# Two blocks of two layers on one core: the last layer on its 256 output tokens, norm sums and the last affine on other engines, constants that wait by tile

## The chip, the core and the metric

The kernel runs on one core of a Trainium2 chip. The metric is the device time of one execution in microseconds (us), the median of several runs. Engines are named as in the profile: PE is TensorE (matmuls; PEld its weight loads), DVE is VectorE, ACT is ScalarE, POOL is GpSimd, and SP is SyncE, whose queue issues the transfers.

## What is computed

The first block is one layer of RWKV-7 and one of gated DeltaNet, each with its SwiGLU, on 256 tokens of width 1024. The second block puts 16 learnt tokens in front (272 tokens) and runs two layers; only the 256 tokens behind those 16 are the output. In short form, from the reference:

```python
x = concat([meta, x], axis=1)                        # 16 + 256 tokens
for i in range(2):
    x = layer_norm(alpha * x + 0.5 * swiglu(x, gate1, up1, down1), ln1)
    z, xbc, dt, fq, fk, fv, ff, cq, ckv, kr = split(x @ w_in)
    y = concat([ssd_mixer(z, xbc, dt), fox_mixer(fq, fk, fv, ff), mla_mixer(cq, ckv, kr)])
    x = layer_norm(alpha * x + y @ w_out, ln2)
    x = layer_norm(alpha * x + 0.5 * swiglu(x, gate2, up2, down2), ln3)
return x[:, 16:]
```

This is its meaning and not its text. The three mixers of a layer are causal: the state mixer, an attention with a forget gate ("fox") and a latent attention ("MLA"). Tokens mix nowhere else. So in the last layer the front 16 tokens are needed as keys, values and state, and not as queries, gates or rows of the later projections.

## The kernel before

Activations lie with features on the partitions, as eight tiles of 128 features by 272 tokens (256 in the first block). A float32 product is made from three: operand and weight are each split into a high and a low part, and high x high, high x low and low x high are summed in PSUM. So one block of 128 output features takes 8 x 3 = 24 matmuls (66 in a down projection of 2816 features), each as wide as the tokens.

- **Weights.** `weight` (L103) loads 128x1024 values by SP, ACT casts the high part (L108), and DVE, or POOL where `onpool` says so, subtracts to the low part (L111). Three raw buffers and four of each part go round. For the first four blocks of each SwiGLU the low parts are made on POOL (`onpool = 4`, L272).
- **SwiGLU.** `ffn` (L259): 22 pairs of gate and up blocks, two pairs at a time, by `mm3` (L149; its products are L157 to L161 for the first four blocks and L166, L167, L169 for the others), then eight blocks down, straight into a layer norm.
- **Mixer.** `mixer` (L320) projects 20 blocks of features. Four come first; the other 16 are emitted step by step by `project` (L123, matmul L137) among the steps of the gates, latents, states, attentions and the state mixer, in an order that `run_spread` (L750) makes from a list of steps and places. Each attention (`attend`, L523) goes through its units of queries: 16 queries of both heads, then 128 and 128 queries for each head. A unit passes score, turn and apply in three successive steps.
- **Output projection.** L705 to L721; four blocks first, then two and two, in two PSUM banks, with DVE reading a result for the norm at L205.
- **Layer norm.** `layer_norm` (L176). Features lie on partitions, so the mean and the mean square come from matmuls with a matrix of 1/1024 (L212, L213). Before that, POOL adds the eight chunks and their squares together (L191: `sa` the chunks, `qa` the squares, each over chunks 0 to 6), so that only the sum and the last chunk go to TensorE. Four more products that nobody reads follow (L215). Then ACT takes the square of the mean (L217), Ln and Exp (L219, L220), DVE subtracts and scales (L221, L235), and with gain and shift ACT writes the high part for the next matmuls (L242), POOL the norm's result (L249), DVE the low part (L232).
- **From the first block to the second.** The last norm of the first block also copies the 16 front tokens into its results: `front[:, k]`, on ACT (L241) and POOL (L247). `front` lies in the pool `modp`, with the modulation vectors. This pool is closed, and the pool `cst` takes its place in memory (L1730) with mask, rope tables and other constants (L297 to L312).
- **Output.** After the last norm SP stores eight tiles (L1735).

The order of work on an engine's queue is not only that of the program's text: the framework places instructions, so that a weight split or a constant can stand ahead of work that is written before it.

## Time and profile before

| | us |
|---|---|
| runs before | 2275.15, 2273.75, 2267.9 (median 2273.75) |
| span of the profiled execution | 2273.7 |
| mean granted TensorE clock, of full speed | 0.972 |
| PE busy, of the span | 2121.1 |
| DVE, ACT, POOL busy | 1415.1, 1083.4, 679.0 |

The span runs from the first to the last instruction of the profiled execution; the profile gives no time of its own outside it. A row of the timeline has the start from the beginning of the span, the duration, the engine, the line of the kernel, the operation, output and inputs; in brackets the idle time of the engine before it and what released it. Successive matmuls overlap, so what one costs is the distance between starts. In the table of stages the clock is the granted share of 2.4 GHz.

### The profile page before, as it was taken

How to read it: one execution, taken by the hardware profiler on the slowest of the kernel's cores; microseconds unless marked ns; L12 is line 12 of the kernel's file. 1: busy time of each engine (PE TensorE's matmuls, PEld its weight loads, DVE VectorE, ACT ScalarE, POOL GpSimd, SP SyncE). 2: the span in 40 equal slices, each digit the busy share in tenths (PEclk: the TensorE clock that was granted, in tenths of full speed). 3: DMA queues.
4: the chain of work that ended last, by engine and by line, in shares of the span. 5: the costliest groups of instructions: out<-in, count | busy, mean ns of one | idle time of the engine just before them, and what ended most of it. 6: DMA issues, size and time to landing. Idle time of an engine off the chain costs nothing.

```text
span 2273.7 us, 43912 instructions
## 1 busy us (share of the span) xinstructions
PE 2121.1 (93%) x17673; PEld 1954.6 (86%) x17673; DVE 1415.1 (62%) x2673; ACT 1083.4 (48%) x1955; POOL 679.0 (30%) x626
## 2 busy tenths in 40 slices
PE   5699999988978898999999999899999999998998
PEld 5488888978977787999899987699999998778998
DVE  6877675455587875654554586565455448665544
ACT  2344444334465545454444464554444536455442
POOL 1625203795464315704201310400230032022003
PEclk9799999999997999999999999999999999999999
DMA  6433222566544322765554432255446553224543
GB/s 248 141 99 115 75 75 86 204 236 214 208 152 149 127 84 88 258 201 185 159 174 165 158 117 65 93 168 176 162 146 193 172 173 115 80 84 144 177 167 112
DMA packets 102236, 337.87 MB, mean 149 GB/s; under 512 B 11472, under 2 KB 19472, under 8 KB 102032
## 3 DMA queue, kind: packets, MB, share of 16 engines
q1 hardware_dynamic: 102032, 335.07, 44.1%
q8 instruction: 138, 2.26, 0.4%
q14 instruction: 66, 0.54, 0.1%
HBM read 333.97 MB, written 1.05 MB: 147 GB/s over the span
## 4 chain that ended last, share of the span: by engine, by line
PE 59%; DVE 6%; ACT 2%; issue 2%; POOL 2%; DMA 0%; POOLq 0%; DVEq 0%; ACTq 0%
PE pj L167 14%; PE pj L166 13%; PE pj L169 13%; PE pj L137 6%; PE pj L157 1%; PE pj L158 1%; DVE wl L111 1%; PE yp L586 1%; PE pj L161 1%; PE B L1369 1%; PE sy L636 1%; PE S L547 1%; PE pt L569 0%; ACT wh L108 0%; DVE r L221 0%
## 5 line engine op out<-in xcount | busy, mean ns | idle before, releaser
L111 DVE TENSOR_TENSOR wl<-wr,wh 128x1024 fp32r<-128x1024 f32 (+2 forms) x533 | 642.7, 1215 | 399.4 <-ACT wh L108 216.7
L108 ACT CAST wh<-wr 128x1024 fp32r<-128x1024 f32 (+2 forms) x557 | 555.8, 1001 | 568.6 <-PE pj L167 206.6
L832 POOL TENSOR_TENSOR adaccp<-adaccp,adar 128x512 f32<-128x512 f32 x140 | 209.5, 1497 | 46.5 <-ACT adar L828 19.4
L202 POOL TENSOR_TENSOR x<-x,m 128x272 f32<-128x272 f32 (+1 forms) x42 | 34.5, 858 | 600.6 <-ACT m L199 600.6
L268 DVE TENSOR_TENSOR hh<-sg,pj 128x272 f32<-128x272 f32 (+1 forms) x132 | 56.6, 429 | 149.2 <-PE pj L169 126.2
L830 POOL TENSOR_SCALAR adar<-adar,cond,zcol 128x512 f32<-128x512 f32 x98 | 112.5, 1155 | 34.4 <-DMA adar<-in_ada_dram 34.4
L111 POOL TENSOR_TENSOR wl<-wr,wh 128x1024 fp32r<-128x1024 f32 x24 | 58.1, 2432 | 141.7 <-ACT wh L108 134.2
L191 POOL TENSOR_TENSOR sa<-sa,r 128x272 f32<-128x272 f32 (+1 forms) x40 | 55.6, 1390 | 126.8 <-DVE r L205 126.7
L166 PE MATMUL pj<-s0h,wh 128*128 128x272 f32 (+1 forms) x240 | 69.5, 290 | 16.4 <-ACT wh L108 16.4
L186 ACT ACTIVATE q<-r 128x272 f32<-128x272 f32 (+1 forms) x80 | 33.2, 426 | 98.9 <-DVE r L205 63.6
L167 PE MATMUL pj<-s5l,wh 128*128 128x272 f32 (+1 forms) x240 | 69.5, 290 | 0.0
L166 PE MATMUL pj<-s6h,wh 128*128 128x272 f32 (+1 forms) x240 | 69.3, 289 | 0.0
L167 PE MATMUL pj<-s2l,wh 128*128 128x272 f32 (+1 forms) x240 | 69.2, 288 | 0.0
L167 PE MATMUL pj<-s7l,wh 128*128 128x272 f32 (+1 forms) x240 | 69.2, 288 | 0.0
L167 PE MATMUL pj<-s3l,wh 128*128 128x272 f32 (+1 forms) x240 | 69.1, 288 | 0.0
L167 PE MATMUL pj<-s1l,wh 128*128 128x272 f32 (+1 forms) x240 | 69.1, 288 | 0.0
L166 PE MATMUL pj<-s3h,wh 128*128 128x272 f32 (+1 forms) x240 | 69.0, 288 | 0.0
L167 PE MATMUL pj<-s4l,wh 128*128 128x272 f32 (+1 forms) x240 | 69.0, 288 | 0.0
L169 PE MATMUL pj<-s6h,wl 128*128 128x272 f32 (+1 forms) x240 | 69.0, 288 | 0.0
L166 PE MATMUL pj<-s4h,wh 128*128 128x272 f32 (+1 forms) x240 | 69.0, 288 | 0.0
L166 PE MATMUL pj<-s5h,wh 128*128 128x272 f32 (+1 forms) x240 | 69.0, 288 | 0.0
L167 PE MATMUL pj<-s6l,wh 128*128 128x272 f32 (+1 forms) x240 | 68.9, 287 | 0.0
(1660 smaller groups left out, 7850.5 us busy)
## 6 DMA issues: line engine op xcount, KB each, us to landing
wr<-in_ffn_in_dram SPq DMA_DIRECT2D x264, 512.0 KB, 3.9
wr<-in_ffn_out_dram SPq DMA_DIRECT2D x96, 512.0 KB, 3.5
adar<-in_ada_dram SPq DMA_DIRECT2D x80, 512.0 KB, 3.7
wr<-in_w_in_dram SPq DMA_DIRECT2D x40, 512.0 KB, 3.5
wr<-in_ffn_out_dram SPq DMA_DIRECT2D x48, 384.0 KB, 3.9
wr<-in_gin_dram SPq DMA_DIRECT2D x32, 512.0 KB, 4.2
wr<-in_w_out_dram SPq DMA_DIRECT2D x16, 512.0 KB, 3.5
adaring<-in_ada_dram SPq DMA_DIRECT2D x8, 512.0 KB, 6.1
```

Source lines behind the costliest of these rows:

```text
L108: nc.scalar.copy(h, r)
L111: eng.tensor_tensor(l, r, h.bitcast(F32), op=SUB)
L137: mm(o, a, b, start=(c == 0), stop=(c == 23))
L166: mm(o, wh, xs[k][0], start=(i == 0), stop=False)
L167: mm(o, wh, xs[k][1], start=False, stop=False)
L169: mm(o, w(k)[1], xs[k][0], start=False, stop=(i == K - 1))
L186: nc.scalar.activation(q[k], d[k], AF.Square)
L191: nc.gpsimd.tensor_tensor(a, t[0] if k == 1 else a, t[k], op=ADD)
L202: nc.gpsimd.tensor_tensor(xs[i], xs[i], m0, op=SUB)
L268: nc.vector.tensor_tensor(hh, sg, up, op=MUL)
L830: nc.gpsimd.tensor_scalar(t, src, c, n.zcol, op0=MUL, op1=ADD)
L832: nc.gpsimd.tensor_tensor(acc[e], acc[e], src, op=ADD)
```

## The change

In the last layer a first token `f0 = 16` is passed to the mixer. The query blocks (MLA's latents 4 and 5, fox's 6 and 7) and the gates (16 to 19) are projected for the tokens from `f0` on, the attentions leave out the unit of 16 queries (24 steps instead of 28), the state mixer's rows, the output projection, its norm and the last SwiGLU have 256 tokens, and the output tiles are stored whole. In both layers' mixer norms the additions of `sa` are on DVE, those of `qa` stay on POOL. The affine of the last norm is on ACT. The pool of constants is opened with `reuse_waits="tile"`: its tiles wait for the tiles whose bytes they take, not for the whole pools.

```diff
-    def project(self, name, blocks, xs, T, per):
+    def project(self, name, blocks, xs, T, per, cut=lambda g: 0):
...
-            o = self.ps("pj", T)
+            t0 = cut(g)
+            o = self.ps("pj", T - t0)
...
-                    mm(o, a, b, start=(c == 0), stop=(c == 23))
+                    mm(o, a, b[:, t0:], start=(c == 0), stop=(c == 23))
...
-                    nc.gpsimd.tensor_tensor(a, t[0] if k == 1 else a, t[k], op=ADD)
+                    (sums if sums is not None and i == 0 else nc.gpsimd).tensor_tensor(a, t[0] if k == 1 else a, t[k], op=ADD)
...
-            if not split:
+            if split is None:
+                nc.scalar.activation(xn[k], d[k], AF.Identity, scale=g(k), bias=b(k))
+            elif not split:
                 nc.gpsimd.tensor_scalar(xn[k][:, f:], d[k], g(k), b(k), op0=MUL, op1=ADD)
...
-        T = T2
+        T, TQ = T2, T2 - f0
...
-                units = [(0, 0)] + [(hh, i) for i in (1, 2) for hh in range(2)]
+                units = ([] if f0 else [(0, 0)]) + [(hh, i) for i in (1, 2) for hh in range(2)]
...
-                    mm(yp[rows, s0:], xdt[:sn, i, 64 * h:64 * h + 64], m[:sn], start=(i == 0), stop=(i == 2))
+                    mm(yp[rows, e:], xdt[:sn, i, 64 * h:64 * h + 64], m[:sn], start=(i == 0), stop=(i == 2))
...
-                       (n.project(win, blocks, sp, T, 8), 384 // 8, 0, 1), 
+                       (n.project(win, blocks, sp, T, 8, lambda g: f0 if g in (4, 5, 6, 7) or g > 15 else 0), 384 // 8, 0, 1),
...
-                    outs = [n.ps(t, T) for t in ("pj", "pj", "yp", "bc")[:m]]
+                    outs = [n.ps(t, TQ) for t in ("pj", "pj", "yp", "bc")[:m]]
...
-            return n.layer_norm(out, xs, ISQ2, 0.5e-5, lambda k: P(f"ln2_g{l}", k), lambda k: P(f"ln2_b{l}", k), T,
+            return n.layer_norm(out, [x[:, f0:] for x in xs], ISQ2, 0.5e-5, lambda k: P(f"ln2_g{l}", k), lambda k: P(f"ln2_b{l}", k), TQ,
...
-                                                   bufs=2 if nm not in ("m0", "m2") else 1), (), slow=False)
+                                                   bufs=2 if nm not in ("m0", "m2") else 1), (), slow=False, sums=nc.vector)
...
-        xs, sp = self.mixer(l, xs, sp)
+        f0 = META if last else 0
+        xs, sp = self.mixer(l, xs, sp, f0)
...
-                     lambda k: P(f"ln3_g{l}", k), lambda k: P(f"ln3_b{l}", k), T, None if last else ())
+                     lambda k: P(f"ln3_g{l}", k), lambda k: P(f"ln3_b{l}", k), T - f0, None if last else ())
...
-        with tc.tile_pool(name="cst", bufs=1) as cst:
+        with tc.tile_pool(name="cst", bufs=1, reuse_waits="tile") as cst:
...
-                nc.sync.dma_start(out[k], xs[k][:, META:])
+                nc.sync.dma_start(out[k], xs[k])
```

## Rows read from the trace of the kernel before

**Rows 1.** The page: TensorE's share of the span; the chain that ended last, by engine.
```profile
PE 2121.1 (93%) x17673; PEld 1954.6 (86%) x17673; DVE 1415.1 (62%) x2673; ACT 1083.4 (48%) x1955; POOL 679.0 (30%) x626
...
PE 59%; DVE 6%; ACT 2%; issue 2%; POOL 2%; DMA 0%; POOLq 0%; DVEq 0%; ACTq 0%
```

**Rows 2.** Busy us (instructions) by stage; us, PE, PEld, DVE, ACT, POOL, clock, DMA.
```profile
1894.00:2016.00 122.00, 118.50 (x776) 92.08 (x774) 90.05 (x257) 71.45 (x176) 10.10 (x13) 1.00 0.26 85
2016.00:2070.00 54.00, 43.32 (x282) 37.59 (x281) 31.67 (x60) 27.13 (x42) 29.36 (x25) 0.94 0.31 98
2070.00:2263.00 193.00, 192.94 (x1533) 191.69 (x1531) 96.36 (x120) 87.48 (x120) 19.12 (x19) 1.00 0.49 161
2263.00:2274.00 11.00, 1.58 (x5) 0.59 (x4) 6.01 (x15) 0.63 (x2) 5.15 (x8) 0.73 0.28 96
```

**Rows 3.** Timeline, PE: start us, us, engine, line, op, operands; 272 columns, down-products' ends.
```profile
2193.55 0.29 PE L166 MATMUL pj<-h0h,wh 128*128 128x272 f32 x1
...
2259.88 0.62 PE L212 MATMUL S<-sa,ones1k 128*128 128x272 f32 x2
```

**Rows 4.** The same, PE, 256 columns, in the first block's last SwiGLU.
```profile
1019.82 0.37 PE L166 MATMUL pj<-h0h,wh 128*128 128x256 f32 x1
...
1081.95 0.60 PE L212 MATMUL S<-sa,ones1k 128*128 128x256 f32 x2
```

**Rows 5.** The same, PE, around the score of 16 queries in a fox attention.
```profile
1985.00 0.23 PE L543 MATMUL S<-cum,ident 32*32 32x16 f32 x2
...
1985.77 0.39 PE L137 MATMUL pj<-s0h,wh 128*128 128x272 f32 x1
```

**Rows 6.** Groups by line and shape, 1890 to 2030: xcount | busy us, mean ns.
```profile
L569 PE MATMUL pt<-ident,att 64*16 64x64 f32 x4 | 0.9, 219 | 0.0
```

**Rows 7.** Timeline, PE, end of the last output projection and what follows.
```profile
2045.51 0.29 PE L717 MATMUL pj<-yo3h,wl 128*128 128x272 f32 x1
2053.15 1.27 PE L212 MATMUL S<-sa,ones1k 128*128 128x272 f32 x2 [7.35 <-POOL sa L191]
```

**Rows 8.** Groups on POOL, 2030 to 2057, with idle before them.
```profile
L111 POOL TENSOR_TENSOR wl<-wr,wh 128x1024 fp32r<-128x1024 f32 x4 | 9.8, 2449 | 0.0
...
L191 POOL TENSOR_TENSOR sa<-sa,r 128x272 f32<-128x272 f32 x5 | 4.9, 977 | 0.1
...
L191 POOL TENSOR_TENSOR sa<-r,r 128x272 f32<-128x272 f32 x1 | 0.9, 908 | 11.1 <-DVE r L209 11.1
```

**Rows 9.** Groups on DVE, 2030 to 2050.
```profile
L209 DVE TENSOR_TENSOR r<-r,m 128x272 f32<-128x272 f32 x7 | 6.4, 921 | 0.1
...
L200 DVE TENSOR_TENSOR r<-r,m 128x272 f32<-128x272 f32 x1 | 0.4, 433 | 0.0
```

**Rows 10.** Timeline, ACT, the first block's last norm.
```profile
1087.78 0.30 ACT L312 CAST identR<-ident 128x128 fp32r<-128x128 f32 x1 [4.56 <-POOL x L247]
1087.99 0.38 ACT L217 ACTIVATE m<-S 128x256 f32<-128x256 f32 x1
...
1090.51 0.60 ACT L242 ACTIVATE s0h<-r,par 128x256 fp32r<-128x256 f32 x1 [0.79 <-DVE r L235]
```

**Rows 11.** The same, POOL.
```profile
1087.54 0.21 POOL L247 COPY x<-front 128x16 f32<-128x16 f32 x1
```

**Rows 12.** The same, PE.
```profile
1083.30 0.67 PE L213 MATMUL S<-q,ones1k 128*128 128x256 f32 x2
...
1091.16 0.60 PE L157 MATMUL pj<-s0h,wh 128*128 128x272 f32 x1 [4.49 <-ACT s0h L242]
...
1102.07 0.29 PE L161 MATMUL pj<-s0l,wh 128*128 128x272 f32 x1
```

**Rows 13.** Timeline, POOL, the tail.
```profile
2268.06 2.88 POOL L249 TENSOR_SCALAR x<-r,par 128x272 f32<-128x272 f32 x4 [0.39 <-DVE r L235]
```

**Rows 14.** The same, DVE.
```profile
2266.32 0.68 DVE L235 TENSOR_TENSOR r<-r,y 128x272 f32<-128x272 f32 x1
...
2267.28 1.74 DVE L235 TENSOR_TENSOR r<-r,y 128x272 f32<-128x272 f32 x4
```

More of the change, by code (lines that the diff above doesn't have):

```diff
@@ L174, in lnexp, with layer_norm @@
             self.nc.scalar.preload_act_table_set("natural_log_exp_and_others")
-    def layer_norm(self, psums, xs, scale, eps, g, b, T, t_, split=None, front=None, slow=True, direct=0):
+    def layer_norm(self, psums, xs, scale, eps, g, b, T, t_, split=None, front=None, slow=True, direct=0, sums=None):
         nc, ap = self.nc, self.actp
@@ L318, in rsq, with mixer @@
         return y
-    def mixer(self, l, xs, sp):
+    def mixer(self, l, xs, sp, f0):
         n, nc, P = self.n, self.n.nc, self.n.P
-        T = T2
+        T, TQ = T2, T2 - f0
         tc = self.n.tc
@@ L395, in bcast, with rms_in @@
                 return ps
-            def rms_in(chunks, ones, g, name, tags, out):
-                ps = n.ps("sy", T)
+            def rms_in(chunks, ones, g, name, tags, out, w=T):
+                ps = n.ps("sy", w)
                 raws, sq = [], []
                 for c in chunks:
-                    r = tt_("rr", bufs=3)
+                    r = tt_("rr", bufs=3)[:, :w]
                     nc.scalar.copy(r, c)
-                    q = tt_("rq", bufs=2)
+                    q = tt_("rq", bufs=2)[:, :w]
                     nc.scalar.activation(q, c, AF.Square)
@@ L413, in rms_in @@
                     nc.vector.scalar_tensor_tensor(r, r, g(i), y, op0=MUL, op1=MUL)
-                    out.append(n.split(kp, f"{name}{i}", r, T, tag=tags[i]))
+                    out.append(n.split(kp, f"{name}{i}", r, w, tag=tags[i]))
                 yield
@@ L440, in latents @@
                     yield
-                yield from rms_in(pcq, self.o256, lambda i: P(f"mqg{l}", i), "cqn", ["yo0", "yo1"], cqn)
+                yield from rms_in(pcq, self.o256, lambda i: P(f"mqg{l}", i), "cqn", ["yo0", "yo1"], cqn, TQ)
             fq, fk = [kt("fq0"), kt("fq1")], [kt("fk0"), kt("fk1")]
@@ L455, in take_v @@
                 return done
-            fox_blocks = [[(6 + c, lambda o, c=c: nc.scalar.mul(fq[c], o, -0.125)), (8 + c, lambda o, c=c: nc.scalar.copy(fk[c], o)),
+            fox_blocks = [[(6 + c, lambda o, c=c: nc.scalar.mul(fq[c][:, f0:], o, -0.125)), (8 + c, lambda o, c=c: nc.scalar.copy(fk[c], o)),
                            (10 + c, take_v(c))] for c in range(2)]
@@ L596, in attend @@
                         key = (4 if fox else 6) + c
-                        ys[key] = n.split(kp, f"yo{key}", yp, T)
+                        ys[key] = n.split(kp, f"yo{key}", yp[:, f0:], TQ)
                     yield
@@ L602, in mixer @@
             xsn = [kt(f"xs{c}") for c in range(4)]
-            zs = [kt(f"zs{c}") for c in range(4)]
+            zs = [kt(f"zs{c}")[:, :TQ] for c in range(4)]
             xdt = kp.tile([128, 3, 512], F32, name="xdt")
@@ L633, in finish @@
                     s0, sn = STT[i]
+                    e = max(s0, f0)
                     rows = slice(64 * (h % 2), 64 * (h % 2) + 64)
-                    (nc.gpsimd if i in [] else nc.vector).tensor_tensor(m[:sn], m[:sn], cbm[h // 4][i][:sn], op=MUL)
-                    mm(yp[rows, s0:], xdt[:sn, i, 64 * h:64 * h + 64], m[:sn], start=(i == 0), stop=(i == 2))
+                    nc.vector.tensor_tensor(m[:sn], m[:sn], cbm[h // 4][i][:sn, e - s0:], op=MUL)
+                    mm(yp[rows, e:], xdt[:sn, i, 64 * h:64 * h + 64], m[:sn], start=(i == 0), stop=(i == 2))
                 for c in range(4):
                     yp = n.ps("sy", T)
-                    ysum[c] = kt(f"ys{c}")
+                    ysum[c] = kt(f"ys{c}")[:, :TQ]
                     for hh in range(2):
@@ L644, in ssd @@
                         for i, (s0, sn) in enumerate(STT):
[L645 to L646 removed]
+                            e = max(s0, f0)
+                            m = tt_(f"ssm{i}", T - s0, 2)[:, e - s0:]
+                            nc.vector.tensor_scalar(m[:sn], bc[:sn, e:], toks[:sn, i, h:h + 1], 0.0, op0=SUB, op1=MIN)
                             nc.scalar.activation(m[:sn], m[:sn], AF.Exp)
@@ L672, in norms @@
                     nc.vector.scalar_tensor_tensor(ysum[c], ysum[c], P(f"ssdg{l}", c), y, op0=MUL, op1=MUL)
-                    ys[c] = n.split(kp, f"yo{c}", ysum[c], T)
+                    ys[c] = n.split(kp, f"yo{c}", ysum[c], TQ)
             def chain(*gens):
@@ L695, in mixer @@
             run_spread((gates(), 6, 0, 0.142), (latents(), 7, 0, 0.15), (states(), 10, 0.088, 0.409), (when(lambda: len(cqn) > 1, heads), 9, 0.15, 0.3),
-                       (n.project(win, blocks, sp, T, 8), 384 // 8, 0, 1),
-                       (chain(when(lambda: "q" in have, lambda: mla(0)), mla(1), when(lambda: 10 in have, lambda: fox(0)), when(lambda: 11 in have, lambda: fox(1))), 28, 0.307, 0.874),
+                       (n.project(win, blocks, sp, T, 8, lambda g: f0 if g in (4, 5, 6, 7) or g > 15 else 0), 384 // 8, 0, 1),
+                       (chain(when(lambda: "q" in have, lambda: mla(0)), mla(1), when(lambda: 10 in have, lambda: fox(0)), when(lambda: 11 in have, lambda: fox(1))), 24 if f0 else 28, 0.307, 0.874),
                        (when(lambda: 15 in have and "s" in have, ssd), 33, 0.565, 0.919))
```

30 lines of the change are left out of this document (14 added, 16 removed).

## The prediction

> **What bounds the kernel now.** I read the page first: TensorE is busy for 93% of the span and holds 59% of the chain that ended last; no other engine has more than 6% of that chain [rows 1]. Then the busy time by stage for the last layer, to see where TensorE is not the bound [rows 2]. The reader should see four kinds of stage. In the last SwiGLU (2070 to 2263) TensorE is busy for 192.94 of 193 us at the full clock: only fewer or cheaper matmuls count there. In the mixer (1894 to 2016) it is 118.50 of 122, so nearly the same. In the stretch from the output projection to the next SwiGLU (2016 to 2070) it is 43.32 of 54, so 10.7 us are waits. In the tail (2263 to 2274) it does nothing, and every us is a latency. Last come the instructions in order of time around those waits. The profiled span is 2273.7 us and the median of the runs is 2273.75, so the sum is made against 2273.7 and stands for the median without a correction.
>
> **Part by part.**
>
> **1. 256 columns in the last SwiGLU.** It issues 44 x 24 = 1056 matmuls up and 8 x 66 = 528 down. The same 528 down-products stand in the trace in both widths: 272 columns run from 2193.55 to 2259.88, 66.33 us or 125.6 ns each [rows 3]; 256 columns, in the last SwiGLU of the first block, from 1019.82 to 1081.95, 62.13 us or 117.7 ns each [rows 4]. The difference is 7.95 ns a matmul. The lower bound is 16 columns at 2.4 GHz, 6.67 ns. 1584 x 7.95 = **12.6 us** (10.6 at the lower price). ACT and VectorE get narrower instructions too, but they are idle half of this stage and are costed at nothing; TensorE covers them.
>
> **2. The last mixer.** Eight of the projection's blocks narrow: 192 x 7.95 ns = 1.5 us; the 24 matmuls of the MLA queries give 0.2. Four attentions lose the block of 16 queries. In a fox attention its score takes TensorE from 1985.00 to 1985.77, 0.77 us [rows 5]; in MLA it has a third of these matmuls, so about 0.3 (an estimate from that row). Its transpose is 219 ns [rows 6], and two small products follow, so about 0.5 more each (also an estimate from that row). 2 x 0.77 + 2 x 0.3 + 4 x 0.5 = 4.1. Together 5.8 us of TensorE's work. The stage has 3.5 us of waits already [rows 2], and with fewer steps between a score and the use of its result some more will show, on VectorE's side above all (90 of 122 us). I take **5.0**; the ends are 1.7 (only the narrower products count) and 6.5 (some waits on the removed block go as well). The narrower norms and sums of the state mixer are under 0.3 us and are in this.
>
> **3. The last output projection.** 192 matmuls x 7.95 = 1.5 us. But behind it TensorE waits 7.35 us for GpSimd [rows 7], and ahead of it for the state mixer's norms; a faster projection only lengthens a wait that something else ends. I take **0.6**, between 0 and 1.5.
>
> **4. Norm sums on VectorE, in the mixers' norms of both layers.** After its last projection matmul TensorE waits 7.35 us and is released by GpSimd's sum [rows 7]. GpSimd is without a gap in that stretch: five of the six additions of the sum at 0.98 us and one at 0.91, 5.8 us, the additions of squares, and four weight splits of 2.45 us for the next SwiGLU [rows 8]. The change takes the 5.8 us out of this queue. The additions of squares stay there, behind the same splits, so the last of them is late next; it moves forward by up to 5.8 us. On VectorE six additions of 433 ns, the price of an undisturbed subtraction of the same shape [rows 9], come to 2.6 us. They wait for nothing but VectorE's own subtraction. Queued behind them are the next read of a PSUM bank, for which TensorE waits, and the splits of the projection's weights. They run while TensorE is still in the projection, and VectorE gets time back, as its subtractions now average 921 ns beside a busy GpSimd against 433 [rows 9]. I take **5.8 us** for each layer, 11.6. The lower end is 5.8 - 2.6 = 3.2 each (VectorE's additions all end up on the path); the upper 8.3 each, if the last squares come right after the projection: the 7.35 us wait nearly gone, and the four pairs of sum matmuls that run from 2053.15 at half price, the clock having fallen in the wait, run at the full clock (a pair takes 1.27 us there [rows 7] and 0.67 undisturbed [rows 12], overlapped ends included; about 1 us over the four).
> What row and rule say differ here. The rows give a drop from a GpSimd queue that has no gap. The Trainium skill, Perfetto Trace Analysis, section Optimizing Scalar/DVE Operations, warns that GpSimd and VectorE share an SBUF read port, so moving work between the two may not help. By that rule the sum would be the first rival's.
>
> **5. The constants.** The second block's constants reuse the memory of the first block's modulation, in which the 16 front tokens lie. With one wait for the whole pool, ACT's cast of the identity waits 4.56 us for the last GpSimd copy of those tokens, and the square of the mean stands behind it in ACT's queue, at 1087.99 [rows 10]. That copy comes at 1087.54, behind weight splits [rows 11]. The sums of the norm were on TensorE by 1083.30 + 0.67 = 1083.97 [rows 12]. With a wait by tile only the constant on the same bytes as the front tokens waits. I expect that to be the attention mask, the first one allocated: its load then holds SP's queue until 1087.54, as now, with the next weight loads behind it. These are for blocks that TensorE reaches after its first 12 us, so I cost that at nothing; without that cover it would be a load's time. VectorE's memsets go into its idle time. The square then starts at 1083.97 instead of 1087.99, 4.0 us earlier, and the chain to TensorE's first product with it. GpSimd's last split ends at 1087.5, just ahead of that product at 1091.16 - 4.0 [rows 12] and of the eighth, which is the first to need it. On top, TensorE's pause of 4.49 us had the clock down afterwards: the 64 products from 1091.16 to 1102.07 took 10.91 us [rows 12] where 64 x 125.6 ns is 8.0. Of these 2.9 us I count half, since the pause shrinks and does not vanish. 4.0 + 1.5 = **5.5 us**; the ends are 0 (the wait stays, for the bytes of a constant that ACT or VectorE writes) and 6.9.
>
> **6. The last affine on ACT.** Now GpSimd writes the eight results, the last four from 2268.06 for 2.88 us, until 2270.94; VectorE's last product, begun in a group at 2267.28, ends at 2269.02 [rows 13, 14]. On ACT one such instruction is 0.60 us [rows 10]. Without GpSimd beside it VectorE's pair of operations takes about 0.68 instead of 0.96 [rows 14] (an estimate: two of the 433 ns operations of [rows 9], overlapping by a fifth). Four pairs so end 1.1 us sooner, VectorE at 2267.9, and two ACT instructions later it is 2269.1. **1.8 us**, between 1.0 and 2.5. Nothing stands behind these eight in ACT's queue; SP's eight output transfers wait for them instead of GpSimd.
>
> **Sum:** 12.6 + 5.0 + 0.6 + 11.6 + 5.5 + 1.8 = 37.1; 2273.7 - 37.1 = 2236.6, say **2237 us**. All lower ends: 10.6 + 1.7 + 0 + 6.4 + 0 + 1.0 = 19.7, so 2254. All upper ends: 12.6 + 6.5 + 1.5 + 16.6 + 6.9 + 2.5 = 46.6, so 2227.
>
> **Rivals.**
> - **The shared port** (chance 0.2). VectorE's additions and GpSimd's work exclude each other, so that a moved addition saves only 0.98 - 0.43 = 0.55 us: 3.2 us a layer. For it: VectorE's 921 ns beside GpSimd [rows 9]. Against: GpSimd's own additions are the longer ones and leave the queue whole. 2237 + 2 x 2.6 = 2242 us.
> - **The constants still wait** (0.1): another written constant covers the front tokens, or the mask's load holds up weights. 2237 + 5.5 = 2242.5 us.
> - **A matmul's price is its weight load, not its columns** (0.05). For it: weight loads are busy nearly as long as matmuls in the last SwiGLU [rows 2]. Against: [rows 3, 4]. Terms 1 and 3 and 1.7 of term 2 go, 14.9 us: 2252 us.
> - **The waits of both norms go altogether** (0.1): the upper ends of terms 4 and 5, 2237 - 5.0 - 1.4 = 2231 us.
> - **Slower: the clock in the last mixer** (0.02). Fewer matmuls and more waits could let TensorE's clock fall to 1.2 GHz there. By [rows 12] a product costs 0.2 us then, some 0.1 more. To lose the 37 us won elsewhere, 370 products, half of the stage's, must run so; at 450 it is 8 us slower, 2282. Against: the granted clock is 1.00 there and the waits are 3% [rows 2].
> - **The cut is not what decides** (0.03): its gains return as waits elsewhere, and the time stays within 0.3%, 2273.
>
> **How the numbers follow.** 0.3%, about 7 us, is what a measurement of this kernel can tell from no change. My forecast holds 0.5, with 2231 to 2244 around it. The range reaches over the rivals that are faster by less and the upper ends: 2226 to 2252. Faster 0.95, same 0.03, slower 0.02.
>
> **What would show it.** Right: the last down-products 117 to 118 ns apart; TensorE's wait behind the projections 1 to 3 us in both layers, and still ended by GpSimd, now by an addition of squares; ACT's square of the mean before 1085 with no release by a GpSimd copy, and the products after it back at the full clock sooner; ACT's last affine about 1.8 us earlier in the tail. Wrong: a wait of over 4 us left behind the projections (the port), the square still near 1088 (the constants), the mixer's waits above 5 us (term 2).

## The result, and the profile after

The changed kernel takes 2248.31 us (median of four runs, 2246.88 to 2252.43) against 2274.45 for the kernel before in the same session (four runs, 2267.9 to 2279.2). The ratio is 0.9882, interval 0.9866 to 0.9897: 26 us faster, inside the range, with the forecast at 37. The profiled execution took 2252.43 us and its span is 2250.6 us.

The page of the changed kernel, the counterpart of [rows 1]:

```profile
PE 2106.1 (94%) x17621; PEld 1942.6 (86%) x17621; DVE 1417.2 (63%) x2665; ACT 1085.1 (48%) x1955; POOL 658.6 (29%) x606
...
PE 57%; DVE 6%; ACT 2%; POOL 2%; issue 1%; DMA 1%; ACTq 0%; SPq 0%; DVEq 0%; POOLq 0%
```

The same four stages as in [rows 2], in the changed kernel (us, then busy us of PE, PEld, DVE, ACT, POOL, then clock):

```profile
1889.70:2010.20 120.50, 113.68 (x722) 89.72 (x721) 86.33 (x239) 69.31 (x167) 8.55 (x13) 0.97 0.27 86
2010.20:2059.60 49.40, 42.85 (x284) 37.13 (x284) 35.70 (x67) 27.35 (x43) 25.70 (x20) 0.93 0.34 107
2059.60:2242.10 182.50, 182.44 (x1535) 181.17 (x1534) 95.75 (x121) 85.88 (x120) 18.65 (x19) 1.00 0.52 171
2242.10:2250.60 8.50, 1.41 (x5) 0.59 (x4) 4.63 (x14) 4.94 (x10) 0.00 (x0) 0.79 0.36 124
```

The last SwiGLU gave most and is still all TensorE. The mixer has 4.8 us less of TensorE's work (113.68 against 118.50) and is only 1.5 us shorter: its waits went from 3.5 to 6.8 us.

For the comparison I cut both traces at three kinds of TensorE instructions: the mean's first product in a norm (m0), the first sum product behind a norm's projection (S), and the first product with an operand's low part in the next SwiGLU or mixer (lo). Each row below is a difference of two such starts.

| stretch, us | before | after | gain |
|---|---|---|---|
| start to S of the first block's last norm (nothing changed in it) | 1081.95 | 1087.36 | -5.4 |
| S to lo: start of the second block | 20.12 | 14.80 | 5.3 |
| first mixer, lo to m0 | 139.54 | 138.43 | 1.1 |
| its norm, m0 to lo | 37.49 | 35.93 | 1.6 |
| norm between the layers, S to lo | 16.26 | 14.88 | 1.4 |
| last mixer, lo to m0 | 138.52 | 136.59 | 1.9 |
| its norm, m0 to lo | 37.46 | 33.23 | 4.2 |
| last SwiGLU, lo to S | 190.25 | 179.42 | 10.8 |
| tail, S to the end | 13.82 | 11.63 | 2.2 |

The other stretches agree within 0.1 us. The gains from the second row on make 28.5 us, of which 2.5 (first mixer, norm between the layers) are in stretches whose work did not change. The first row differs between executions of the same instructions: over all profiles here it is 1073.6 to 1087.4 us. So I compare stretches, and use medians for the whole. The SwiGLU stretches repeat within 0.1 us from one profile to the next; stretches with waits in them do not, and what one pair of profiles says of them is checked against other profiles with the same instructions further down.

TensorE's waits in the two mixer norms, from the changed kernel's timeline (first layer, then last), to be set against the 7.35 us of [rows 7]:

```profile
1455.24 0.56 PE L722 MATMUL pj<-yo6h,wh 128*128 128x272 f32 x1 [3.92 <-DVE r L207]
...
1464.59 0.72 PE L214 MATMUL S<-qa,ones1k 128*128 128x272 f32 x2 [1.18 <-POOL qa L193]
...
2035.09 0.36 PE L722 MATMUL pj<-yo6h,wh 128*128 128x256 f32 x1 [2.52 <-DVE r L207]
...
2044.58 0.70 PE L214 MATMUL S<-sa,ones1k 128*128 128x256 f32 x2 [2.07 <-DVE sa L193]
```

The wait behind the projection fell from 7.35 to 1.2 and 2.1 us. But a new one stands inside the projection, for VectorE's read of a PSUM bank: 3.9 and 2.5 us (0.66 us there before). That takes back 3.3 and 1.9 us. In the first layer the clock takes another 1.4 us: the SwiGLU's first 64 products behind the norm need 9.68 us where they needed 8.31.

The start of the second block, and the tail's affine, changed kernel, timeline (the counterparts of [rows 10 to 13]):

```profile
1086.02 7.01 POOL L111 TENSOR_TENSOR wl<-wr,wh 128x1024 fp32r<-128x1024 f32 x3 [1.86 <-PE pj L170]
...
1088.90 0.39 ACT L219 ACTIVATE m<-S 128x256 f32<-128x256 f32 x1
...
1089.83 1.40 DVE L223 TENSOR_TENSOR r<-r,S 128x256 f32<-128x256 f32 x4
1091.15 2.16 DVE L237 TENSOR_TENSOR r<-r,y 128x256 f32<-128x256 f32 x1
...
1094.00 0.39 PE L158 MATMUL pj<-s0h,wh 128*128 128x272 f32 x1 [1.93 <-ACT s0h L244]
...
2243.09 4.74 ACT L251 ACTIVATE x<-r,par 128x256 f32<-128x256 f32 x8 [0.49 <-DVE r L237]
```

The square of the mean starts 1.5 us behind the first sum product, where it was 6.0 us behind. But VectorE's first product of the norm now takes 2.16 us, beside GpSimd's splits. The four subtractions just ahead of it run beside the same splits and take 1.40 us together: they read the mean, S, from PSUM, where the product has both inputs in SBUF.

### The profile page after: what moved, and what is told of

Its sections match the earlier page's. It is cut to its first block, busy times and chain, and to the rows that moved or that the text cites. A ratio compares the mean times of both kernels' runs of the same rounds, so it can differ in the third digit from the quotient of the medians.

```text
span 2250.6 us, 43790 instructions
## 1 busy us (share of the span) xinstructions
PE 2106.1 (94%) x17621; PEld 1942.6 (86%) x17621; DVE 1417.2 (63%) x2665; ACT 1085.1 (48%) x1955; POOL 658.6 (29%) x606
## 4 chain that ended last, share of the span: by engine, by line
PE 57%; DVE 6%; ACT 2%; POOL 2%; issue 1%; DMA 1%; ACTq 0%; SPq 0%; DVEq 0%; POOLq 0%
PE pj L167 13%; PE pj L168 13%; PE pj L170 13%; PE pj L138 6%; DVE wl L111 1%; PE pj L158 1%; PE yp L591 1%; PE pj L159 1%; PE B L1377 1%; PE pj L162 1%; PE sy L642 1%; POOL adaccp L840 1%; DMA wr<-in_ffn_in_dram 1%; PE S L552 1%; PE pt L574 0%
## 5 line engine op out<-in xcount | busy, mean ns | idle before, releaser
L167 PE MATMUL pj<-s0h,wh 128*128 128x256 f32 (+1 forms) x240 | 69.5, 289 | 16.6 <-ACT wh L108 16.5
L188 ACT ACTIVATE q<-r 128x256 f32<-128x256 f32 (+1 forms) x80 | 32.8, 423 | 99.5 <-DVE r L207 63.7
L170 PE MATMUL pj<-s6h,wl 128*128 128x256 f32 (+1 forms) x240 | 69.0, 287 | 0.0
L168 PE MATMUL pj<-s5l,wh 128*128 128x256 f32 (+1 forms) x240 | 68.9, 287 | 0.0
L167 PE MATMUL pj<-s6h,wh 128*128 128x256 f32 (+1 forms) x240 | 68.9, 287 | 0.0
L170 PE MATMUL pj<-s0h,wl 128*128 128x256 f32 (+1 forms) x240 | 68.7, 286 | 0.2 <-DVE wl L111 0.2
L168 PE MATMUL pj<-s7l,wh 128*128 128x256 f32 (+1 forms) x240 | 68.7, 286 | 0.0
L170 PE MATMUL pj<-s1h,wl 128*128 128x256 f32 (+1 forms) x240 | 68.7, 286 | 0.0
L167 PE MATMUL pj<-s4h,wh 128*128 128x256 f32 (+1 forms) x240 | 68.6, 286 | 0.0
L167 PE MATMUL pj<-s5h,wh 128*128 128x256 f32 (+1 forms) x240 | 68.5, 286 | 0.0
L168 PE MATMUL pj<-s1l,wh 128*128 128x256 f32 (+1 forms) x240 | 68.5, 285 | 0.0
```

Of the source, the lines that this page charges most:

```text
L167: mm(o, wh, xs[k][0], start=(i == 0), stop=False)
L168: mm(o, wh, xs[k][1], start=False, stop=False)
L170: mm(o, w(k)[1], xs[k][0], start=False, stop=(i == K - 1))
L188: nc.scalar.activation(q[k], d[k], AF.Square)
```

## The experiments

All twelve start from the changed kernel, and each is compared with the kernel before on the same chip; line numbers are those of the run that a row or an edit belongs to.

### Each part undone by itself

Four kernels, each with one part put back:

```diff
no_sums:
-    ... (), slow=False, sums=nc.vector)
+    ... (), slow=False)
no_tile:
-        with tc.tile_pool(name="cst", bufs=1, reuse_waits="tile") as cst:
+        with tc.tile_pool(name="cst", bufs=1) as cst:
no_affine:
-                nc.scalar.activation(xn[k], d[k], AF.Identity, scale=g(k), bias=b(k))
+                nc.gpsimd.tensor_scalar(xn[k], d[k], g(k), b(k), op0=MUL, op1=ADD)
no_cut:
-        f0 = META if last else 0
+        f0 = 0
...
-                nc.sync.dma_start(out[k], xs[k])
+                nc.sync.dma_start(out[k], xs[k][:, META:])
```

> The changed kernel with the additions of both mixer norms back on GpSimd. Theory (the additions are worth what the two norms show): the stretch from the mean's first product to the first low-part product, 35.9 us in layer 0 and 33.2 in layer 1 of the changed kernel, goes back to 37.5 in layer 0 and to about 36.5 in layer 1, the wait behind the projection is over 6 us again, and the time is 3 to 6 us longer. Rival (layer 1 won by its narrower columns alone and the additions are worth nothing there): layer 1 stays at 33 to 34.5, and the time is at most 2 us longer.

> The changed kernel with the constants' pool waiting for whole pools again; every engine has the same instructions in the same order. Theory: ACT's cast waits for GpSimd's last copy of the front tokens again, and the stretch from the sums to the first low-part product, 14.8 us in the changed kernel, is 20.1 again: 5.3 us longer, half of it because the products run at the lower clock. Rival (the three GpSimd splits would hold VectorE's first scaling about as long as the wait did): 2.5 us longer or less.

> The changed kernel with the last affine back on GpSimd. Theory: from the last norm's sums to the end 13.4 to 13.8 us instead of 11.6, 1.8 to 2.2 longer. Rival (the 256 columns and not the engine shortened the tail): under 0.7 longer.

> The changed kernel with all 272 tokens in the last layer. Theory: the last SwiGLU takes 10.8 us more from its first low-part product to its sums, the products before it 0.7, the mixer about 2 and the norm about 1: 14 to 15 us longer in all. Rival (a product costs its weight load, not its columns): at most 4.

| | median, us | ratio to before | the stretch that the part is in |
|---|---|---|---|
| no_sums | 2251.15 | 0.9896 [0.9872, 0.992] | mixer norms 37.45 and 35.30 (with the part: 35.93 and 33.23) |
| no_tile | 2254.99 | 0.9913 [0.9887, 0.9938] | start of the block 18.73 (14.80) |
| no_affine | 2249.96 | 0.9888 [0.9861, 0.9915] | tail 12.79 (11.63) |
| no_cut | 2263.76 | 0.9959 [0.9943, 0.9974] | last mixer 141.83 (136.59), last SwiGLU 190.25 (179.42) |

In the totals only the cut stands clear of the changed kernel's interval. Against the one profile of the changed kernel the stretches give the sums 1.5 and 2.1 us (5.8 each were forecast), the waits by tile 3.9, the affine 1.2, the cut 10.8 in the SwiGLU. Of these only the SwiGLU's figure needs no second look. Some runs, of this section and of those below, leave a mixer norm's instructions as they are in the changed kernel (after), and the stretches differ:

| norm, m0 to lo, us | sums on VectorE | sums on GpSimd |
|---|---|---|
| first layer, 272 columns | 33.30 no_cut, 35.31 mix_steps, 35.84 wide_latents, 35.93 after, 36.49 no_tile, 36.54 no_affine | 37.45 no_sums, 37.49 before |
| last layer, 256 columns | 32.87 no_affine, 33.23 after, 34.68 no_tile, 36.01 mix_steps, 36.01 wide_latents | 35.30 no_sums |

So the move of the sums was worth 0.9 to 4.2 us in the first layer and between -0.7 and 2.4 us in the last, and 1.5 and 2.1 are one draw from that. Even the best profile is below the 5.8 that was forecast. Two things make most of the spread: which of two weight splits starts first (next section), and the clock behind the norm, where the same 64 products of the next SwiGLU take 8.3 or 9.5 to 9.7 us (7.6 or 9.2 at 256 columns). The waits by tile are alike: 2.6 of the 3.9 us are the wait itself (4.50 us in no_tile, 1.93 in the changed kernel), the rest is clock. The affine's move gives 1.2 us at 256 columns, and 1.8 at 272 (no_cut's tail is 12.0 us, 13.8 before).

Not all expectations were met. In no_sums the first layer came back to 37.45 as expected, the last only to 35.30 (36.5 was expected, 33 to 34.5 by the rival), with a wait of 5.45 us instead of over 6. no_tile and no_affine came out between theory and rival. no_cut is 15.5 us above the changed kernel by the medians, a little more than expected, and the rival (at most 4, a product costs its weight load) falls. Without the wait by tile ACT's cast of the identity waits again, as in [rows 10]:

```profile
1089.58 0.30 ACT L316 CAST identR<-ident 128x128 fp32r<-128x128 f32 x1 [4.57 <-POOL x L249]
```

The last mixer without the cut is longer than it was before, 141.83 against 138.52 us, with the same instructions there; its clock tells why, further down.

### Why the sums gained so much less than was forecast

The changed kernel's first mixer norm, timeline of GpSimd and VectorE around the new wait:

```profile
1451.12 2.54 POOL L111 TENSOR_TENSOR wl<-wr,wh 128x1024 fp32r<-128x1024 f32 x1
...
1451.39 3.36 DVE L111 TENSOR_TENSOR wl<-wr,wh 128x1024 fp32r<-128x1024 f32 x1
...
1454.67 0.78 DVE L207 SCALAR_TENSOR_TENSOR r<-pj,x 128x272 f32<-128x272 f32 x2
...
1456.46 1.69 POOL L193 TENSOR_TENSOR qa<-qa,q 128x272 f32<-128x272 f32 x2 [2.80 <-ACT q L188]
```

In the last layer of the same execution VectorE's split comes first:

```profile
2033.39 1.21 DVE L111 TENSOR_TENSOR wl<-wr,wh 128x1024 fp32r<-128x1024 f32 x1
...
2033.56 3.27 POOL L111 TENSOR_TENSOR wl<-wr,wh 128x1024 fp32r<-128x1024 f32 x1 [0.38 <-ACT wh L108]
```

VectorE's split takes 1.21 us undisturbed, GpSimd's 2.35. In the first layer VectorE's starts 0.27 us behind a GpSimd split and ends 1.1 us after that one's end (1453.66): it stood still for as long as that one ran. In the last layer it is GpSimd's that is stretched. The read of the PSUM bank stands behind the split in VectorE's queue, TensorE waits for that read, and GpSimd then waits 2.8 us for a square, which hangs on the same read. Two theories: VectorE and GpSimd exclude each other (P), or VectorE's queue has the added sums in a bad place (O).

```diff
dve_splits (low parts of the first four blocks behind a mixer on VectorE):
-                self.onpool = 4 if j == 0 else 0
+                self.onpool = early if j == 0 else 0
...
+                     ... T - f0, None if last else (), early=0)
dve_splits_pool_sums: the same, and
-    ... (), slow=False, sums=nc.vector)
+    ... (), slow=False)
late_sums (each sum on VectorE behind a later PSUM read):
+                for j in {4: (1,), 5: (2,), 6: (3, 4), 7: (5,)}.get(k, ()):
+                    with self.tc.issue_after(read.ins):
+                        sums.tensor_tensor(sa, d[0] if j == 1 else sa, d[j], op=ADD)
m0_psum (the subtracted mean read from PSUM):
-                    nc.vector.tensor_tensor(r, r, m0, op=SUB)
+                    nc.vector.scalar_tensor_tensor(r, m0p, -8.0, r, op0=MUL, op1=ADD)
```

> The low parts of the first four weight blocks of the SwiGLU behind a mixer are made on VectorE instead of GpSimd, in both layers; the sums stay on VectorE. Theory P (VectorE's instructions of the norm are slow because GpSimd's splits run beside them): VectorE's reads of the projection fall back to 0.45 us, TensorE's wait before the projection's seventh block falls from 3.9 (first layer) and 2.5 us (second) to under 1, the stretch from the mean's first product to the next SwiGLU's first low-part product is 30 to 32 us in the first layer (35.9 now) and 28 to 30 in the second (33.2), the time 2240 to 2243 us. Theory O (VectorE's order: the added sums stand ahead of the PSUM reads in its queue): the waits stay at 2 us or more, the stretches within 1 us of now, the time 2247 to 2249. A third way: four splits of about 1.1 us each on VectorE land in front of the norm's own work there and the wait only changes its name: the stretches 1 to 4 us longer, 2250 to 2256.

> The same four low parts on VectorE, and the norm's sums back on GpSimd. Theory P: with the splits off GpSimd its additions follow their inputs closely (12 x 0.6 to 1.0 us against a projection of some 25 us), so that it matters little where the sums are made: within 2 us of the run with the sums on VectorE, 2240 to 2245. Theory O: this is the faster of the two by 2 us or more, since VectorE has nothing in front of its reads. If moving the sums is worth the forecast 5.8 us a layer whatever else GpSimd does, this is 8 to 12 us slower than the run with the sums on VectorE.

> The sums stay on VectorE, but each addition is put behind a later read of the projection in VectorE's queue (the last two behind the last read); GpSimd's splits stay. Theory O: TensorE's wait before the seventh block goes from 3.9 and 2.5 us to under 1; what comes back is a wait behind the last block for the two late additions (about 1 us), so the stretches are 33 and 31 us, the time 2243 to 2245. Theory P: VectorE is held by the splits beside it, not by its order: waits within 1 us of now, the time 2247 to 2250.

> In the mixers' norms VectorE's subtraction of the first mean reads it where TensorE left it, in PSUM, instead of ACT's copy in SBUF; the splits stay on GpSimd and the sums on VectorE. Theory P, made narrower (GpSimd and VectorE exclude each other instruction by instruction, but only where VectorE's instruction takes both inputs from SBUF, as the reads of the projection, which take one from PSUM, run at 0.41 us beside a GpSimd split): these subtractions, 0.4 to 2.25 us now, all take 0.4 to 0.5 us, while the sums and the low parts beside a split stay at up to 3.4 us; the two norm stretches, 35.9 and 33.2 us, each get 1 to 3 us shorter, the time 2243 to 2246 us. Rival (VectorE is slowed beside GpSimd whatever it reads): the subtractions stay at up to 2 us, the stretches within 0.5 us of now, 2247 to 2249 us.

| | median, us | ratio to before | norm stretches, us | last norm, m0 to S | exclusive work there (estimate) |
|---|---|---|---|---|---|
| before | | | 37.49, 37.46 | 21.0 | 26.6 |
| after | 2248.31 | 0.9882 [0.9866, 0.9897] | 35.93, 33.23 | 18.3 | 24.6 |
| late_sums | 2251.81 | 0.9894 [0.9873, 0.9916] | 37.13, 35.32 | 18.9 | 24.6 |
| dve_splits | 2246.3 | 0.9879 [0.985, 0.9907] | 32.78, 31.64 | 16.5 | 20.0 |
| dve_splits_pool_sums | 2241.04 | 0.9855 [0.9835, 0.9875] | 33.46, 31.56 | 16.0 | 21.9 |
| m0_psum | 2238.52 | 0.9835 [0.9815, 0.9855] | 32.33, 32.07 | 14.4 | 21.6 |

Late sums do take the wait inside the projection away in the last layer (none over 0.3 us left there), and a longer one appears behind the projection:

```profile
2042.98 1.22 PE L221 MATMUL S<-qa,ones1k 128*128 128x256 f32 x2 [6.95 <-POOL qa L193]
```

The stretches got no shorter (37.13 and 35.32), so theory O falls as the reason for the small gain. As for the wait inside the projection it is half right, and P's sign, waits within 1 us of now, failed. VectorE's own queue makes 1.8 us of that wait in the first layer and 2.5 in the last: so much stays when GpSimd's splits are gone (dve_splits), or when VectorE's split starts first (1.80 in no_cut's first layer, 2.52 above). Where GpSimd's starts first the stretched split adds 2.1 (3.92 above, 4.68 in mix_steps' last layer).

Theory P holds in direction. With the splits off GpSimd the norms take 31.6 to 33.5 us. They are 1.6 to 3.2 us shorter than in the changed kernel's profile, and all but one shorter than every profile with the splits on GpSimd in the table above. In the stretches it then matters by less than 1 us where the sums are made. The medians differ by 5.3 us in favour of GpSimd, which is theory O's sign; but in the profiled executions 6.7 us of difference lie in the first block, where the two kernels are the same, and from S on dve_splits is the faster by 2.3. Against its numbers it missed: the first layer's stretch is 32.8 instead of at most 32, the last one's 31.6 instead of at most 30, and a wait of 1.8 and 2.5 us inside the projection stayed, as VectorE's own eight splits and six sums now fill its queue. Its time, 2246.3 us, isn't told from the changed kernel's. That of the run with the sums on GpSimd is lower in all four executions, though the intervals of the two ratios still touch.

The run with the mean in PSUM shows the mechanism in one line. Groups on VectorE in the last norm, changed kernel first, then with the mean in PSUM:

```profile
L211 DVE TENSOR_TENSOR r<-r,m 128x256 f32<-128x256 f32 x7 | 6.4, 923 | 0.1
...
L207 DVE SCALAR_TENSOR_TENSOR r<-pj,x 128x256 f32<-128x256 f32 x6 | 2.4, 417 | 1.7 <-PE pj L724 1.6
```

```profile
L211 DVE SCALAR_TENSOR_TENSOR r<-pt,r 128x256 f32<-128x256 f32 x7 | 2.8, 417 | 0.1
...
L193 DVE TENSOR_TENSOR sa<-sa,r 128x256 f32<-128x256 f32 x5 | 5.7, 1138 | 0.1
```

The subtraction goes from 923 to 417 ns, the price of the reads from PSUM (L207), which were never stretched; the sums, which still take both inputs from SBUF, stay long, 1138 (1041 in the changed kernel). In its first layer the two splits of the fence above start within 0.03 us of each other, in the other order, and there GpSimd's is the long one:

```profile
1445.72 1.22 DVE L111 TENSOR_TENSOR wl<-wr,wh 128x1024 fp32r<-128x1024 f32 x1
...
1445.75 3.43 POOL L111 TENSOR_TENSOR wl<-wr,wh 128x1024 fp32r<-128x1024 f32 x1 [0.25 <-ACT wh L108]
```

So part of that layer's 3.6 us comes from this turn of luck: against the profiles in which VectorE's split also starts first (33.30 in no_cut's first layer, 32.87 and 33.23 in the last) the mean in PSUM gains 0.8 to 1.2 us a norm. The time, 2238.52 us, came out below the expected 2243 to 2246. Of the 9.8 us that its median lies below the changed kernel's, the profiles show 4.3 from S on; the rest is not accounted for by the edit. That it is the operand and not the new form of the instruction is shown by the start of the second block above, where TENSOR_TENSOR took 1.40 us for four with an operand in PSUM and 2.16 for one without. A VectorE instruction with both inputs in SBUF and a GpSimd instruction exclude each other for their whole length, and the first one wins (3.36 against 1.21 us for VectorE's split; 3.43 and 3.27 against 2.35 for GpSimd's). The Trainium skill, SBUF — State Buffer, section SBUF: two separate sides, calls the pair of ports that the two share an exclusive lock, held by whichever starts first for the whole instruction; these rows agree.

The last column adds what must pass one at a time in the last norm, at the undisturbed prices that these traces show: a GpSimd addition 0.74 us, its split 2.35, a VectorE operation 0.42 (0.43 at 272 columns), its split 1.21. For the changed kernel: 6 x 0.74 + 4 x 2.35 + 14 x 0.42 + 4 x 1.21 = 24.6; before, 12 additions on GpSimd and 8 subtractions: 26.6. The move takes 2.0 us off this sum. It orders the kernels by and large and not exactly: late_sums, dve_splits and m0_psum lie out of line, and no_sums, at 26.5 by this sum, reached S after 17.6 us, sooner than the changed kernel. So it is a guide to the size of what a move can give, and no price.

### Where the last mixer's gain went

```diff
mix_steps (an empty step at the head of each attention):
+                if f0:
+                    yield
...
-  ... 24 if f0 else 28, 0.307, 0.874)
+  ... 28, 0.307, 0.874)
wide_latents:
-  ... lambda g: f0 if g in (4, 5, 6, 7) or g > 15 else 0)
+  ... lambda g: f0 if g in (6, 7) or g > 15 else 0)
-  ... ["yo0", "yo1"], cqn, TQ)
+  ... ["yo0", "yo1"], cqn)
-  ... for w in wuq)], cqn)
+  ... for w in wuq)], [(a[:, f0:], b[:, f0:]) for a, b in cqn])
```

> The last mixer's attention chain gets its four removed steps back as empty ones, so that it is spread over 28 steps as before; the work stays cut. Theory: the cut took 5.3 us of TensorE's work from the last mixer, and 3.4 us came back as waits on VectorE because the steps lie otherwise against the projection; with the old spread the waits fall from 7.7 to some 4.3 us, the last mixer's stage from 136.6 to 133 to 134 us, and the time to 2244 to 2246. Rival: the waits are of the state mixer's own chain on VectorE, whatever the attention's steps are: 136 to 137 us, the time 2247 to 2249.

> One part of the cut undone in the last mixer: the two blocks of MLA's query latents and their norm are 272 columns wide again; the queries made from them, the attentions, the gate, the output projection and the SwiGLU stay at 256. Theory: in the changed kernel the narrower latents' product by their norm stands ahead of the state mixer's first decay differences in VectorE's order and waits 1.5 us there for ACT's root, TensorE waits 2.6 us behind it (1.0 before), and after that wait the clock falls (0.85 granted in the stage's second 20 us, 1.00 before). With the order as before the wait for the differences is 1.0 to 1.5 us, the clock 0.95 to 1.00 there, and the last mixer's stage 131.5 to 134 us instead of 136.6; the time 2243 to 2246. Rival: the clock falls there whatever this order is (it is at 0.84 with the whole cut undone too): 136 to 137.5 us, and the time 2247 to 2250.

mix_steps: 2246.98 us, ratio 0.9877 [0.9858, 0.9896]; the mixer 135.28 us instead of 136.59. That is between the theory and its rival, and it shows neither: the nine other profiles with this mixer's work, without the empty steps, take 135.18 to 136.84 us there. The norm behind it got longer (36.01 against 33.23), for the reason of the last section and with 9.2 us instead of 7.6 for the 64 products behind it: there GpSimd's split starts 0.14 us ahead of VectorE's, and TensorE waits 4.68 us.

```profile
2024.29 2.41 POOL L111 TENSOR_TENSOR wl<-wr,wh 128x1024 fp32r<-128x1024 f32 x1
...
2024.43 3.35 DVE L111 TENSOR_TENSOR wl<-wr,wh 128x1024 fp32r<-128x1024 f32 x1
```

The larger part lies early in the mixer. The changed kernel, timeline of VectorE and TensorE, and its second 20 us there by busy time:

```profile
1907.98 0.88 DVE L418 SCALAR_TENSOR_TENSOR rr<-rr,par,rsy 128x256 f32<-128x256 f32 x2 [1.51 <-ACT rsy L321]
1908.78 0.88 DVE L653 TENSOR_SCALAR ssm<-bc,toks 128x256 f32<-128x256 f32 x3
...
1909.81 0.56 PE L398 MATMUL bc<-cumh,identR 64*128 64x272 f32 x1 [2.62 <-DVE ssm L653]
```

```profile
1909.70:1929.70 20.00, 17.76 (x108) 15.74 (x109) 16.55 (x31) 12.31 (x29) 2.44 (x4) 0.85 0.40 129
```

The latents' product by their root (L418) stands ahead of the state mixer's decay differences (L653) in VectorE's queue and waits 1.5 us for ACT's root; TensorE needs the differences out of their bank and waits 2.6 us. In the kernel before the differences stood first and TensorE waited 1.0. Then the clock is at 0.85, so part of these 20 us ran at 1.2 GHz. With the latents alone 272 columns wide again, the differences stand ahead of the product as before:

```profile
1902.95 0.89 DVE L653 TENSOR_SCALAR ssm<-bc,toks 128x256 f32<-128x256 f32 x3
...
1903.99 0.36 PE L398 MATMUL bc<-cumh,identR 64*128 64x272 f32 x1 [1.07 <-DVE ssm L653]
1904.77 0.91 DVE L418 SCALAR_TENSOR_TENSOR rr<-rr,par,rsy 128x272 f32<-128x272 f32 x2
```

```profile
1905.10:1925.10 20.00, 19.67 (x138) 17.14 (x137) 18.94 (x43) 15.14 (x37) 3.18 (x5) 1.00 0.30 100
```

The mixer takes 131.94 us, 6.6 less than before and 4.65 less than in the changed kernel: the theory's range, hit. It is well clear of the ten profiles with narrow latents, and best_c, below, repeats it (131.63). Width and order came back together here, and narrow latents in the old order were not run: that the order does it is argued, not shown. In the total, 2245.38 us, ratio 0.9869 [0.9852, 0.9885], little of it shows, since the norm behind lost 2.8 us (36.01) to the same unlucky order of the splits as in mix_steps.

The clock itself isn't settled. In these 20 us it was 0.83 to 0.91 in all ten profiled kernels with narrow latents and 1.00 in three of the four with wide ones. The fourth is the run without the cut: old order, a wait of 1.00 us, and still

```profile
1908.20:1928.20 20.00, 19.39 (x119) 17.33 (x119) 16.38 (x34) 12.46 (x30) 2.57 (x4) 0.84 0.26 91
```

That run prices the clock: 141.83 - 138.52 = 3.3 us for the same instructions at 0.84 instead of 1.00. By this price some 3 of the 4.65 us would be clock. The whole mixer's busy times, changed kernel and then wide latents, say less:

```profile
1889.73:2026.32 136.59, 128.88 (x827) 102.34 (x826) 94.65 (x257) 77.63 (x181) 10.54 (x14) 0.98 0.26 84
```

```profile
1885.13:2017.07 131.94, 127.41 (x827) 100.31 (x826) 94.69 (x257) 77.23 (x181) 10.30 (x14) 1.00 0.27 87
```

TensorE is idle for 7.7 us in the one and 4.5 in the other, so 3.2 of the 4.65 us are waits and 1.5 are left for busy time at the lower clock, less the narrower columns. The clock's share lies somewhere between 1.5 and 3 us (an estimate); what tips the clock at this place stays open.

### The findings together

best_a puts all the second block's low parts on VectorE (`early=0` in its other SwiGLUs too), the sums back on GpSimd and reads the mean from PSUM. best_c adds the wide latents. Beside the edits shown above:

```diff
-  lambda k: P(f"ln1_g{l}", k), lambda k: P(f"ln1_b{l}", k), T)
+  lambda k: P(f"ln1_g{l}", k), lambda k: P(f"ln1_b{l}", k), T, early=0)
```

> All of the second block's low parts on VectorE (those at its start and between its layers too), the mixers' sums back on GpSimd, and the first mean read from PSUM. By theory P this takes GpSimd's 2.5 us splits away from all norms: against the run with the splits behind the mixers on VectorE and the sums on GpSimd (2241.0) the norms lose another 0.5 to 1 us each, and the start of the block the 1.1 us by which VectorE's first product there is stretched now: 2237 to 2240 us. Rival: at the block's start three splits of 1.1 us land in VectorE's queue in front of the norm's subtractions, and the start gets 1 to 3 us longer: 2241 to 2244 us.

> The two findings together: the second block's low parts on VectorE, the mixers' sums on GpSimd, the first mean read from PSUM (2235.0 us by itself), and MLA's query latents of the last mixer 272 columns wide (by itself 4.7 us off the last mixer's stage). If they are independent: the last mixer's stage 131.5 to 132.5 us (136.7 in the first alone), its norm stretch still 31 to 32.5 us although VectorE's order there moves, the time 2229 to 2232 us. Rival: the last mixer's gain goes into the norm's stretch behind it, as in the run with the wide latents alone (33.2 to 36.0 us there): that stretch 34 to 35 us, 2232 to 2235.

| | median, us | ratio to before | start of block | norms | last mixer |
|---|---|---|---|---|---|
| best_a | 2235.0 | 0.9828 [0.9807, 0.9848] | 13.67 | 32.18, 31.70 | 136.73 |
| best_c | 2236.06 | 0.9808 [0.9782, 0.9834] | 13.66 | 31.19, 29.02 | 131.63 |

best_a came out 2 us below its range. The block's start gained the expected 1.1 us: VectorE's first product there takes 0.42 us instead of 2.16, and the stretch to TensorE's first product is 5.52 us instead of 6.64. Of the norms the first got 1.3 us shorter than in dve_splits_pool_sums, the last no shorter. In best_c the stretches came out as expected or better: in its profiled execution (2228.45 us) the work from S on takes 1148.2 us, against 1157.4 in best_a, 1163.2 in the changed kernel and 1191.75 before. Its median does not show that: its five runs spread from 2222.41 to 2237.18, three of them at 2236 to 2237, which have no trace but a mean granted clock of 0.971 to 0.972 against 0.978 and 0.980 in the two short ones, and the expectation of 2229 to 2232 is missed. So best_c is not told from best_a; both beat the kernel before, and lie below the changed kernel's 2248.31.

## Why the prediction was right or wrong

By its own steps, with what the stretches measured:

| term | forecast | measured | |
|---|---|---|---|
| 1, last SwiGLU | 12.6 | 11.3 | 7.13 ns a matmul instead of 7.95 |
| 2, last mixer | 5.0 | 1.9 | 6.6 with the latents wide |
| 3, last output projection | 0.6 | 1.7 | by one pair of profiles |
| 4, norm sums | 11.6 | 3.6 | 1.5 + 2.1; other profiles 0.9 to 4.2 and -0.7 to 2.4 |
| 5, constants | 5.5 | 5.3 | 2.6 of wait, 2.8 of clock |
| 6, last affine | 1.8 | 2.2 | 1.2 the move, 1.0 narrower instructions |
| sum | 37.1 | 26.0 | and 2.5 in unchanged stretches |

The time fell inside the range, and the mechanisms of terms 1, 5 and 6 are right. But the forecast itself is 11 us too fast, and 11.1 us of that is terms 4 (8.0) and 2 (3.1); the range held because its slow end, 2252, was drawn over the rivals. Of these the shared port, at 2242, names what happened.

- **Term 1 is right in kind and a tenth too large.** 10.83 us over 1584 - 64 matmuls is 7.13 ns (the other 64 lie in the norm's stretch). The up-products gained 7.65 ns each, as the rows said; the down-products stand (2238.97 - 2175.88) / 528 = 119.5 ns apart, not the 117.7 of [rows 4], with no wait between them. Why they are slower than in the first block wasn't tried.
- **Term 2 was too large.** TensorE's busy time went down by 5.3 us (134.18 to 128.88), about as costed. The step that failed is taking 5.0 of 5.8: the waits to come on VectorE's side were named but priced at 0.8 us, and they were 3.4, most of them in the first 40 us, where the narrow latents stand in another order on VectorE's queue; and the clock, put down as a rival of 2 in 100 that would have to lose 37 us, came as a loss of 1.5 to 3 us. The sign named for it, waits above 5 us in the mixer, did come (6.8). With the latents wide the gain is 6.6, just above the upper end.
- **Term 3** seems to have got more than its upper end (1.5): the last norm's stretch is 4.2 us shorter, 2.1 of it by the sums and 0.46 by the 64 products of term 1. That leaves 1.7, but by the one pair before and no_sums. With the sums on VectorE the narrower columns move the stretch from 34.48 (no_cut) to between 32.87 and 36.01, so that the premise of a longer next wait was wrong is not shown.
- **Term 4 is the step that failed.** "The change takes the 5.8 us out of this queue" priced GpSimd's additions at 0.98 us and took the queue behind as GpSimd's alone. The 0.98 were 0.74 us of work and a lock, and so were the 921 ns of VectorE's subtractions [rows 9]. In a stretch where both engines pass one at a time, moving an addition saves 0.74 - 0.42 = 0.32 us, 1.9 for six, inside the spread that the profiles show. VectorE's additions were not free either: "They run while TensorE is still in the projection" left out the PSUM reads queued behind them, for which TensorE now waits 1.8 and 2.5 us (0.66 before), 2.1 more where GpSimd's split starts first. The shared port was the first rival, with the wrong price (0.55 an addition, from the stretched 0.98); what the Trainium skill, Perfetto Trace Analysis, section Optimizing Scalar/DVE Operations, warns of is what happened: most of the 5.8 us did not come. The sign that was named for it, over 4 us left behind the projection, did not come: the wait moved into the projection.
- **Term 5** is right in its sum and less so in its parts. The square no longer waits. The first product came 6.64 us behind S instead of 9.21, 2.6 gained instead of 4.0, since VectorE's first product was locked for 1.7 us, a collision that the text did not look for. The clock gave 10.91 - 8.16 = 2.8 us for the 64 products; in other profiles with the same wait they take 9.5 to 9.7, so this part is 1.2 to 1.5, or 2.8.
- **Term 6** holds: the move alone is worth the forecast 1.8 us at 272 columns (no_cut).

## What to carry to other kernels

A duration read from a busy stretch is not a price: where GpSimd and VectorE work side by side out of SBUF, add up both engines' undisturbed prices as one queue, and expect a move between them to be worth only the difference. An operand left in PSUM takes a VectorE instruction out of that queue (923 to 417 ns here). After any change of widths, look at the order in which an engine's queue now stands: here narrowing two blocks of latents cost 4.65 us, with two VectorE instructions swapped, longer waits and a lower clock. And before a stretch with waits in it is used as a price, read it in several profiles of the same instructions: here it moved by 3 us.

## What had not been expected of the hardware

- Which of two instructions starts first decides who pays: splits that start 0.03 to 0.27 us apart cost VectorE 2.2 us or GpSimd 1.1, and in the norm's stretch about 2 us, up to 3 with the clock behind it.
- With the same wait of 1.92 us ahead of them, the 64 products at the start of the second block take 8.2 us in four profiles and 9.5 to 9.7 in six others.
- The clock fell to 0.84 in the last mixer of a kernel whose instructions and waits there were as before (1.00).
